# A22's negated copy for the first sum of a pair: made by GpSimd instead of ScalarE

## The chip, the core and the metric

The kernel runs on one core of a Trainium2 chip. The core has a matrix engine (TensorE, PE in the profile), a vector engine (VectorE, DVE), an engine for activations and copies (ScalarE, ACT), a general one (GpSimd, POOL) and a queue that only starts transfers (SyncE, SP). Each works through its own queue of instructions and waits on semaphores for the others. PEld in the profile is the loading of weights into TensorE. Transfers between the main memory and the on-chip memory are issued by SP, ACT or POOL and run beside the engines.

The metric is the device time of one execution in microseconds (us), lower being better.

## What is computed

Two layers of a small transformer work on 256 tokens of an image ("lat") and 256 tokens of context ("cx"), 1024 features each, in float32. The first layer mixes tokens by a short convolution, the second by attention. Before and after the mixer stands a feed-forward network, so there are four; in the second layer the context ends at the attention, and the last network works on the image tokens alone.

```python
def _modulate(t, g, shift, scale):
    return _rms(t, g) * (1 + scale) + shift

def _swiglu(h, w13, w2):
    gte, up = jnp.split(h @ w13, 2, axis=-1)
    return (jax.nn.silu(gte) * up) @ w2
...
    mod = (jax.nn.silu(c) @ mod_w[i] + mod_b[i]).reshape(bsz, 3, 3, 1, D_MODEL)
...
    lat = lat + 0.5 * mod[:, 0, 2] * _swiglu(_modulate(lat, norm_g[i, 0], ...), ffn_w13[i, 0], ffn_w2[i, 0])
```

The change lies in the product `h @ w13` of the first three networks: 1024 features by 2 x 2816 hidden columns.

## The kernel before

**Precision.** A float32 product is made of three TensorE products. Each operand is split into a rounded part "hi" and the rest "lo" (`split`, L107): ACT copies the source with rounding (L108), DVE subtracts that copy from the source (L109). `mm3` (L133) issues hi x hi (L137), hi x lo (L138) and lo x hi (L139) into one accumulator. So each weight tile costs one ACT and one DVE pass before TensorE can use it.

**A network.** `ffn` (L766) works on the 22 blocks of 128 hidden columns in three thirds of 8, 7 and 7. For each block the gate and the up product are made, then silu(gate) * up, and at the end of a third `project` (L575) multiplies the blocks by `w2` and adds the result to the tokens (`finish`, L559). Work of a slower kind runs between: the modulation vectors are made on DVE (L179) in units that the loops hand out (`tick`).

**A pair.** In the first three networks most blocks are made by the class `Pair` with seven products of half-size blocks in place of eight, in the manner of Strassen and Winograd. The weights of a block are cut into A11 and A12 (first half of the features; up and gate columns) and A21 and A22 (second half), the tokens into B blocks and their sums T1 to T4. Two tiles of 128x1024 hold a pair's weights: `r2` gets A22 and A12 by one transfer (through `load_raw`, L104), and the right half of `r1` gets A11 by another (L693). The left half of `r1` is made in two steps: a copy of A22 times -1 (L695), then a transfer that POOL issues, which adds A21 from memory to what lies there (L696). So it holds A21 - A22. `sums(0)` subtracts it from A11 on DVE (L715) and splits both halves into S1 and S2 (`keep`, L703). `sums(1)` makes split copies of A22 itself (`split_far`, L111: two passes on ACT, L113 and L114, and a second adding transfer by POOL, L115), subtracts S2's raw form from both halves of `r2` on DVE (L723), and splits the result into S3 and S4.

The products follow in this order: `head` (A11 and A12; ACT then copies the first product to `sg`, L740), `five` (S1 by T1; ACT copies it to `gm`, L746), `six` (S2 by T2, which adds to the accumulator that L740 copied; S4, which adds to the one that L746 copied), and for the pair before `seven` (S3; DVE L757) and `four` (A22; DVE L763 and the split of the result). There are 56 pairs, and so 56 negations.

**Buffers and order.** Raw weight tiles have 8 buffers ("wr"), split tiles 4 each ("wh" and "wl"), A22's split copies 2 each ("w4h" and "w4l"). A weight buffer is free again when its last reader is done. The order on each engine is written out by hand only for the first stage and for the attention heads (`manual_schedule`); elsewhere a planner of the tile layer places the instructions of several pairs between each other by costs of its own. Loads, negations and adding transfers of later pairs therefore stand in the queues among the products and copies of earlier ones.

**Other users of POOL.** POOL issues the two adding transfers of each pair. In the attention stage, which has no pairs, it also multiplies 128x512 tiles by a scalar (L1300).

Of the kernel before, what the change touches and what calls it, by code (L numbers as in the profile page):

```python
# [12 lines left out]
AF = mybir.ActivationFunctionType  # L13
ALU = mybir.AluOpType
# [6 lines left out]
T2 = 2 * S  # L21
# [26 lines left out]
def hybrid_kernel(ctx: ExitStack, tc: tile.TileContext, a: dict, out: bass.AP):  # L48
    nc = tc.nc
# [12 lines left out]
    def nm(s):  # L62
        uid[0] += 1
        return f"{s}{uid[0]}"
# [15 lines left out]
    for q in range(4):  # L80
# [10 lines left out]
        out=const.tile([P, 1], F32, name="silu", tag="silu"), in_=eps_t, func=AF.Silu  # L91
# [10 lines left out]
    def load_raw(src, n=1024):  # L102
        raw = wp.tile([P, 1024], F32, name=nm("wr"), tag="wr", bufs=8)
        nc.sync.dma_start(raw[:, :n], src)  # L104
        return raw

    def split(hi, lo, src):  # L107
        nc.scalar.activation(out=hi, in_=src, func=AF.Copy)  # L108
        return nc.vector.tensor_tensor(out=lo, in0=src, in1=hi.bitcast(F32), op=ALU.subtract)  # L109
# [7 lines left out]
    def half():  # L117

        return tuple(
            wp.tile([P, 1024], F32R, name=nm(t), tag=t, bufs=4) for t in ("wh", "wl")  # L120
        )
# [198 lines left out]
    class Plain:  # L320


        def __init__(self):
            self.t = [(hot("hh"), hot("hl")) for _ in range(KT // 2)]
# [357 lines left out]
    class Pair:  # L682
# [6 lines left out]
        def __init__(self, src, h):  # L689
            self.h, self.w, self.src = h, {}, src  # L690
            r2 = load_raw(src[:, 1024:2048])
            r1 = wp.tile([P, 1024], F32, name=nm("wr"), tag="wr", bufs=8)
            nc.sync.dma_start(r1[:, T2:], src[:, T2:1024])  # L693

            nc.scalar.activation(out=r1[:, :T2], in_=r2[:, :T2], func=AF.Copy, scale=-1.0)  # L695
            nc.gpsimd.dma_start(out=r1[:, :T2], in_=src[:, :T2], accum_op=ALU.add)  # L696
            self.raw = [r1, r2]
            ts = half()
            for i, key in enumerate(("A11", "A12")):
                self.w[key] = [t[:, i * T2 : i * T2 + T2] for t in ts]  # L700
                split(*self.w[key], self.raw[i][:, T2:])
# [185 lines left out]
    for k in range(KT):  # L887
# [5 lines left out]
        out=sb1, in0=modb[:, 0, KT : 2 * KT], scalar1=1.0, scalar2=None, op0=ALU.add  # L893
# [175 lines left out]
    for m in range(KT):  # L1069
# [4 lines left out]
        for c0, c1 in ((0, S), (S, T2)) if m == 0 else ((0, T2),):  # L1074
# [18 lines left out]
            out=d2[:, :, 1:], in0=u2[:, :, : S - 1], scalar=convk[:, 0, m : m + 1],  # L1093
# [3 lines left out]
            out=d2[:, :, : S - 1], in0=u2[:, :, 1:], scalar=convk[:, 2, m : m + 1],  # L1097
# [152 lines left out]
    for kv in range(KVH):  # L1250
# [8 lines left out]
        out=scq, in0=rq[:, :16], scalar1=float(P) ** -0.5, scalar2=None, op0=ALU.mult  # L1259
# [202 lines left out]
```

## Time and profile before

| | before |
|---|---|
| time, median of 3 runs | 1584.83 us (1580.87 to 1585.39) |
| time of the profiled execution | 1582.14 us |
| its span | 1580.4 us |
| TensorE busy | 1558.5 us, 99% |
| VectorE busy | 1279.5 us, 81% |
| ScalarE busy | 801.8 us, 51% |
| GpSimd busy | 123.1 us, 8% |
| memory traffic | 263.52 MB, mean 167 GB/s |
| mean granted TensorE clock | 0.996 |

How to read the lines quoted below. In the order of time, a line gives its start in us from the start of the span, its length in us, engine, source line, operation, output and inputs, shape and count; brackets at the end tell how long the engine stood idle before it and whose work ended that. In the groups, a line gives line, engine, operation, names, shapes and count, then busy us and mean ns of one, then the idle time before these instructions and what ended it. In the list of waits, the numbers are total us, how often, and the longest. In the view by stretches, a line gives the stretch, its length, the busy us (with the count of instructions) of PE, PEld, DVE, ACT and POOL, the granted TensorE clock, the share of DMA and GB/s. "fp32r" is the rounded form of float32 that the splits produce. Matmuls overlap, so a busy share of PE near 100% says that it hardly waits, not that it runs at its peak.

### The profile page before, as it was taken

How to read it: one execution, taken by the hardware profiler on the slowest of the kernel's cores; microseconds unless marked ns; L12 is line 12 of the kernel's file. 1: busy time of each engine (PE TensorE's matmuls, PEld its weight loads, DVE VectorE, ACT ScalarE, POOL GpSimd, SP SyncE). 2: the span in 40 equal slices, each digit the busy share in tenths (PEclk: the TensorE clock that was granted, in tenths of full speed). 3: DMA queues.
4: the chain of work that ended last, by engine and by line, in shares of the span. 5: the costliest groups of instructions: out<-in, count | busy, mean ns of one | idle time of the engine just before them, and what ended most of it. 6: DMA issues, size and time to landing. Idle time of an engine off the chain costs nothing. (4 is left out here: it accounts for less than half of the span.)

```text
span 1580.4 us, 26335 instructions
## 1 busy us (share of the span) xinstructions
PE 1558.5 (99%) x10282; PEld 1426.4 (90%) x10282; DVE 1279.5 (81%) x2023; ACT 801.8 (51%) x1345; POOL 123.1 (8%) x132
## 2 busy tenths in 40 slices
PE   9999999999999999999999999999999999999999
PEld 7888998999888899989999899989889889898888
DVE  5978789789998678977987988977968887887676
ACT  5643553554332366446446476446445355674553
POOL 0001101100000000011010001011010002300000
PEclk9999999999999999999999999999999999999999
DMA  9667457555565434674665724665865753256562
GB/s 370 211 178 190 117 155 198 130 170 174 182 203 175 134 81 120 190 176 102 201 166 126 215 67 125 202 163 129 243 158 154 244 162 124 91 183 220 166 202 74
DMA packets 88253, 263.52 MB, mean 167 GB/s; under 512 B 10817, under 2 KB 12609, under 8 KB 88129
## 3 DMA queue, kind: packets, MB, share of 16 engines
q1 hardware_dynamic: 69408, 230.72, 45.6%
q0 software_dynamic: 16128, 29.37, 11.3%
q10 hardware_dynamic: 2592, 1.76, 0.4%
q8 instruction: 80, 1.31, 0.3%
q14 instruction: 45, 0.36, 0.1%
HBM read 259.45 MB, written 1.05 MB: 165 GB/s over the span
## 5 line engine op out<-in xcount | busy, mean ns | idle before, releaser
L109 DVE TENSOR_TENSOR wl<-wr,wh 128x1024 fp32r<-128x1024 f32 (+2 forms) x446 | 455.5, 1045 | 144.7 <-ACT wh L108 123.4
L108 ACT ACTIVATE wh<-wr 128x1024 fp32r<-128x1024 f32 (+2 forms) x446 | 394.1, 912 | 245.5 <-PE py L138 79.3
L179 DVE CUSTOM_DVE_ANT_0 junk<-wr,scbc,modb 128x1024 bf16<-128x1024 f32 x222 | 284.5, 1281 | 31.8 <-DMA wr<-in_modT 29.0
L137 PE MATMUL py<-gh,wh 128*128 128x512 f32 (+1 forms) x570 | 214.3, 376 | 0.0
L138 PE MATMUL py<-gl,wh 128*128 128x512 f32 (+1 forms) x570 | 214.0, 375 | 0.0
L139 PE MATMUL py<-gh,wl 128*128 128x512 f32 (+1 forms) x570 | 213.7, 375 | 0.0
L137 PE MATMUL p<-th,wh 128*128 128x256 f32 x448 | 127.3, 284 | 4.6 <-ACT sg L740 4.6
L139 PE MATMUL p<-th,wl 128*128 128x256 f32 x448 | 127.1, 284 | 0.0
L138 PE MATMUL p<-tl,wh 128*128 128x256 f32 x448 | 127.0, 283 | 0.0
L139 PEld LDWEIGHTS py<-gh,wl 128*128 128x128 f32 x570 | 107.9, 189 | 19.2
L137 PEld LDWEIGHTS py<-gh,wh 128*128 128x128 f32 x570 | 108.0, 190 | 18.2
L138 PEld LDWEIGHTS py<-gl,wh 128*128 128x128 f32 x570 | 108.0, 190 | 18.0
L559 DVE SCALAR_TENSOR_TENSOR x<-py,mod,x 128x256 f32<-128x256 f32 x213 | 94.2, 479 | 34.5 <-PE py L139 23.3
L696 POOL DMA_DIRECT2D wr<-in_w x56 | 48.8, 872 | 829.9 <-ACT wr L695 672.5
L695 ACT ACTIVATE wr<-wr 128x512 f32<-128x512 f32 x56 | 35.2, 629 | 117.5 <-DMA wr<-in_w 80.9
L137 PE MATMUL q<-bh,wh 128*128 128x256 f32 x320 | 91.1, 285 | 2.0 <-ACT gm L746 1.6
L139 PE MATMUL q<-bh,wl 128*128 128x256 f32 x320 | 91.0, 284 | 0.6 <-DVE wl L109 0.6
L137 PEld LDWEIGHTS p<-th,wh 128*128 128x128 f32 x448 | 86.1, 192 | 5.4 <-ACT sg L740 5.0
L138 PE MATMUL q<-bl,wh 128*128 128x256 f32 x320 | 90.7, 283 | 0.0
L138 PEld LDWEIGHTS p<-tl,wh 128*128 128x128 f32 x448 | 86.1, 192 | 0.4
L139 PEld LDWEIGHTS p<-th,wl 128*128 128x128 f32 x448 | 86.1, 192 | 0.0
L108 ACT ACTIVATE gh<-gm 128x512 fp32r<-128x512 f32 x66 | 41.3, 625 | 71.6 <-DVE gm L763 68.0
(304 smaller groups left out, 4065.8 us busy)
## 6 DMA issues: line engine op xcount, KB each, us to landing
wr<-in_modT SPq DMA_DIRECT2D x126, 512.0 KB, 4.8
wr<-in_w SPq DMA_DIRECT2D x120, 512.0 KB, 4.6
wr<-in_w2b SPq DMA_DIRECT2D x64, 448.0 KB, 4.1
wr<-in_w2a SPq DMA_DIRECT2D x32, 512.0 KB, 5.0
wr<-in_w SPq DMA_DIRECT2D x56, 256.0 KB, 4.0
wr<-in_w POOLq DMA_DIRECT2D x56, 256.0 KB, 4.9
w4l<-in_w POOLq DMA_DIRECT2D x56, 256.0 KB, 5.9
pm<-in_mod SPq DMA_DIRECT2D x16, 512.0 KB, 10.2
```

What stands on the lines that cost most here:

```text
L108: nc.scalar.activation(out=hi, in_=src, func=AF.Copy)
L109: return nc.vector.tensor_tensor(out=lo, in0=src, in1=hi.bitcast(F32), op=ALU.subtract)
L137: nc.tensor.matmul(ps, wh, mh, start=first, stop=False, **kw)
L138: nc.tensor.matmul(ps, wh, ml, start=False, stop=False, **kw)
L139: nc.tensor.matmul(ps, wl, mh, start=False, stop=last, **kw)
L179: nc.vector.tensor_tensor_reduce(out=junk, in0=raw[j], in1=scbc[:, v, :], scale=0.5 if ch in (2, 8) else 1.0, scalar=modb[:, l, col : col ...
L559: nc.vector.scalar_tensor_tensor(out=x[:, m, s * S : s * S + S], in0=ps[:, o : o + S], scalar=g[:, m, s : s + 1], in1=x[:, m, s * S : s * ...
L695: nc.scalar.activation(out=r1[:, :T2], in_=r2[:, :T2], func=AF.Copy, scale=-1.0)
L696: nc.gpsimd.dma_start(out=r1[:, :T2], in_=src[:, :T2], accum_op=ALU.add)
```

## The change

GpSimd makes the negated copy. The operation (times -1), the operands, the shape and the transfer that adds to it are the same; no wait or buffer is written differently. After it, the negation stands on L695 to L697, and every line behind it is two further down (the adding transfer is L698, L715 becomes L717, and so on).

```diff
             r1 = wp.tile([P, 1024], F32, name=nm("wr"), tag="wr", bufs=8)
             nc.sync.dma_start(r1[:, T2:], src[:, T2:1024])
 
-            nc.scalar.activation(out=r1[:, :T2], in_=r2[:, :T2], func=AF.Copy, scale=-1.0)
+            nc.gpsimd.tensor_scalar(
+                out=r1[:, :T2], in0=r2[:, :T2], scalar1=-1.0, scalar2=None, op0=ALU.mult
+            )
             nc.gpsimd.dma_start(out=r1[:, :T2], in_=src[:, :T2], accum_op=ALU.add)
             self.raw = [r1, r2]
```

## The prediction

> **What bounds the kernel now.** I read the page's engine shares first, then the chain of waits of PE, then the groups of the changed line, then the order of time on ACT, PE and DVE where PE waits.
>
> ```profile
> span 1580.4 us, 26335 instructions
> ...
> PE 1558.5 (99%) x10282; PEld 1426.4 (90%) x10282; DVE 1279.5 (81%) x2023; ACT 801.8 (51%) x1345; POOL 123.1 (8%) x132
> ...
> L695 ACT ACTIVATE wr<-wr 128x512 f32<-128x512 f32 x56 | 35.2, 629 | 117.5 <-DMA wr<-in_w 80.9
> ```
>
> TensorE bounds nearly every stage: it is idle for 1580.4 - 1558.5 = 21.9 us, so no relief of another engine can bring much more. ACT is half idle, and the removed work, 35.2 us, is worth nothing by itself. But the last row says more: ACT stood idle for 117.5 us right ahead of the 56 negations, 80.9 us of them until the weights landed. An engine runs its queue in order, so whatever stands behind a waiting negation waits with it. Who suffers is told by PE's waits:
>
> ```profile
> PE p L137 <- ACT sg L740: 4.6, 2, 2.9
> PE q L137 <- ACT gm L746: 4.0, 4, 1.8
> ```
>
> PE waits twice for the copy of the first product (L740), 2.9 and 1.7 us, and four times for the copy of S1*T1 (L746), 4.0 us in all: 1.8 once, the other three 2.2, or 0.73 each. All stand where a third of a feed-forward network starts its pairs. First place, ACT's order of time, in two stretches:
>
> ```profile
> 269.32 0.63 ACT L695 ACTIVATE wr<-wr 128x512 f32<-128x512 f32 x1 [7.79 <-DMA wr<-in_w]
> 269.86 1.04 ACT L108 ACTIVATE wh<-wr 128x1024 fp32r<-128x1024 f32 x1
> ```
> ```profile
> 277.55 0.63 ACT L695 ACTIVATE wr<-wr 128x512 f32<-128x512 f32 x1 [3.10 <-DMA wr<-in_w]
> 278.09 1.13 ACT L108 ACTIVATE wh<-wr 128x512 fp32r<-128x512 f32 x2
> 280.73 0.63 ACT L695 ACTIVATE wr<-wr 128x512 f32<-128x512 f32 x1 [1.51 <-DVE wl L109]
> 281.27 0.35 ACT L740 COPY sg<-p 128x256 f32<-128x256 f32 x1
> 282.04 1.07 ACT L108 ACTIVATE wh<-wr 128x1024 fp32r<-128x1024 f32 x1 [0.42 <-ACT sg L740]
> 283.01 0.34 ACT L746 COPY gm<-q 128x256 f32<-128x256 f32 x1
> ```
> ```profile
> 278.50 0.28 PE L139 MATMUL q<-th,wl 128*128 128x256 f32 x1
> 281.68 0.39 PE L137 MATMUL p<-th,wh 128*128 128x256 f32 x1 [2.89 <-ACT sg L740]
> ```
>
> The copy at 281.27 stands directly behind two negations of later pairs, each of which waited for its own load; PE needed it at 278.6. After that stall PE also runs slower:
>
> ```profile
> 283.00:287.00 4.00, 4.00 (x22) 3.77 (x21) 3.00 (x3) 1.67 (x4) 0.00 (x0) 0.57 0.78 164
> ```
> ```profile
> 1168.00:1172.00 4.00, 4.00 (x34) 4.00 (x35) 2.68 (x3) 1.13 (x2) 0.00 (x0) 1.00 0.41 134
> ```
>
> These are two stretches of 4 us in the view by stretches, with matmuls in brackets and the granted clock third from the end: at a clock of 0.57 PE issued 22 matmuls of the form of which it issues 34 at 1.00. The 12 missing ones are 12 x 4.00/34 = 1.4 us.
>
> **The change, part by part.**
>
> *Order.* In the built program PE's and SP's orders are unchanged. ACT loses the 56 negations; in a few places the two A22 copies (L113, L114) move by a neighbour. DVE swaps neighbours in three places; I take that at nothing. POOL gains 56 negations, each right ahead of the DMA that adds to its result, and one setup instruction long before the first. The order of POOL's DMAs stays.
>
> *The negation on POOL.* Its nearest row is the attention stage's multiplication of the same shape, with POOL and DVE side by side there:
>
> ```profile
> L1300 POOL TENSOR_SCALAR pn<-e,r x16: 1553/1565/1867, 1331.9 to 1361.9; 128x512 f32<-128x512 f32 x16
> ```
> ```profile
> 1347.48 3.11 POOL L1300 TENSOR_SCALAR pn<-e,r 128x512 f32<-128x512 f32 x2 [0.95 <-PE pt L1313]
> ```
> ```profile
> 1347.89 0.81 DVE L109 TENSOR_TENSOR wl<-wr,wh 128x512 fp32r<-128x512 f32 x1
> ```
> ```profile
> L109 DVE TENSOR_TENSOR wl<-wr,wh 128x512 fp32r<-128x512 f32 x132 | 85.9, 690 | 26.7 <-ACT wh L108 26.5
> ```
> ```profile
> L715 DVE TENSOR_TENSOR wr<-wr 128x512 f32<-128x512 f32 x56 | 38.4, 685 | 1.0 <-DMA wr<-in_w 1.0
> ```
>
> 56 x 1.565 = 87.6 us on an engine that is busy 123.1 of 1580.4. Where ACT started the negation the moment the load landed, the adding DMA now goes out 1.565 - 0.629 = 0.94 us later; where ACT was late, earlier. Its reader is L715, and the last row says that L715 waited for a DMA 1.0 us in all 56 times: the DMA is covered elsewhere, and 0.94 us late costs nothing. For that one wait (the first pair) I bound it by -1.0 and +0.94 and take 0, since POOL needn't wait for ACT's queue there. If the cover were gone everywhere, it would be 56 x 0.94 = 53 us. Behind a waiting negation on POOL stand the adding DMA, which waited for the same load before, and A22's DMA of an earlier pair (L115), already queued behind that one. SP's loads don't pass POOL.
>
> *What DVE loses beside POOL.* The split at 1347.89 ran inside a POOL operation and took 0.81 us; the mean of its form is 0.690. So 0.12 us is lost per such operation, and a negation of 1.565 us can meet two. That is 56 x 0.12 = 6.7 to 56 x 0.24 = 13.4 us of DVE, which is idle for 300.9 us. PE sees it only where DVE is late already: three places, two negations each, 6 x 0.24 = +1.5 us. Bounds: 0, and the lock below.
>
> *What ACT gains, first place.* Without negations the copy L740 runs behind the halves at 278.09 and before PE asks. Late next is the copy L746: it stands behind L108 at 282.04, which reads DVE's L715:
>
> ```profile
> 270.94 1.23 DVE L109 TENSOR_TENSOR wl<-wr,wh 128x1024 fp32r<-128x1024 f32 x1 [2.04 <-ACT wh L108]
> ...
> 280.89 0.69 DVE L715 TENSOR_TENSOR wr<-wr 128x512 f32<-128x512 f32 x1
> ```
>
> If DVE stayed put, PE would stop again 1.44 us (12 matmuls at 0.12) after 278.62, at 280.06, until 283.4, and nothing would be won: that is the lower end, 0. But DVE itself waited 2.04 us for the split at 269.86, behind a negation that sat 7.79 us. Without it L715 moves from 280.89 to 278.85, L108 to 280.0, the copy to 281.0, and PE restarts at 281.4 instead of 283.4: -2.0 us. A wait of 1.3 us in place of 2.9 should leave the clock alone (the second place waits 1.7 us and the stretch from 1168 has 1.00), so -1.4 us more. Together -3.4; the upper end is 2.9 + 0.3 + 1.4 = -4.6.
>
> The Trainium skill (TensorE: Matmul & The Clock Gate, "What's actually happening") says that the clock is halved after an idle window of about 3.4 us which runs freely, so that the same gap may or may not cost it. The trace agrees: 0.57 over 4 us is 3.4 us at half clock. With the window falling otherwise, the sum would lack its 1.4 us.
>
> *Second place.*
>
> ```profile
> 1159.46 0.63 ACT L695 ACTIVATE wr<-wr 128x512 f32<-128x512 f32 x1 [6.41 <-DMA wr<-in_w]
> 1160.00 1.04 ACT L108 ACTIVATE wh<-wr 128x1024 fp32r<-128x1024 f32 x1
> 1163.38 0.63 ACT L695 ACTIVATE wr<-wr 128x512 f32<-128x512 f32 x1 [2.34 <-DVE x L559]
> 1163.92 1.13 ACT L108 ACTIVATE wh<-wr 128x512 fp32r<-128x512 f32 x2
> 1164.95 0.35 ACT L740 COPY sg<-p 128x256 f32<-128x256 f32 x1
> 1166.54 1.06 ACT L108 ACTIVATE wh<-wr 128x1024 fp32r<-128x1024 f32 x1 [1.24 <-issue]
> 1167.51 0.35 ACT L746 COPY gm<-q 128x256 f32<-128x256 f32 x1
> ```
> ```profile
> 1161.07 1.23 DVE L109 TENSOR_TENSOR wl<-wr,wh 128x1024 fp32r<-128x1024 f32 x1 [1.73 <-ACT wh L108]
> 1162.21 0.87 DVE L559 SCALAR_TENSOR_TENSOR x<-py,mod,x 128x256 f32<-128x256 f32 x2
> 1164.56 1.29 DVE L109 TENSOR_TENSOR wl<-wr,wh 128x512 fp32r<-128x512 f32 x2 [1.47 <-ACT wh L108]
> 1165.77 0.69 DVE L715 TENSOR_TENSOR wr<-wr 128x512 f32<-128x512 f32 x1
> ```
>
> The same picture: DVE waits 1.73 + 1.47 = 3.2 us for splits behind negations. With these gone the first copy no longer waits (-1.7), and L715 is 3.2 us earlier, more than the second copy was late (-0.7). Together -2.4; lower end 0, where the halves' buffers hold ACT instead.
>
> *Third place.*
>
> ```profile
> 702.85 1.29 DVE L109 TENSOR_TENSOR wl<-wr,wh 128x512 fp32r<-128x512 f32 x2 [2.13 <-ACT wh L108]
> ```
>
> One of the three waits of 0.73 us for L746 follows it, and 2.13 us of DVE's lateness are ACT's: -0.7, or 0.
>
> *Sum.* -3.4 - 2.4 - 0.7 + 1.5 = -5.0 us. The profiled execution took 1582.14 us (its span is 1580.4), so 1577.1, rounded to 1577. Its own time is 2.7 us under the median of 1584.83, inside the runs' spread of 1580.87 to 1585.39.
>
> **The rivals.**
>
> *The copies are held by something else.* The halves need buffers that PE's last projection frees, and DVE needn't move when ACT does. Then the new waits replace the old ones, DVE's loss is +1.5 at most, and the time is 1581 to 1584. For it: half of each gain hangs on DVE moving. Against it: DVE's waits name ACT in all three places.
>
> *Slower: POOL shuts DVE out.* Should a negation hold off every DVE operation with two inputs in SBUF for its whole length, DVE loses up to 87.6 us. On the average it has room. At the start of a third it hasn't: two negations fall within 4 us there (277.55, 280.73), 3.1 us of DVE, of which a microsecond may be spare. Nine thirds x 2.1 = +19, less nothing gained: about 1601. It decides from (3.4 + 2.4 + 0.7)/9/2 = 0.36 us lost per negation, against 0.12 to 0.24 by the row. Against it: the split at 1347.89 started and ended inside a POOL operation.
>
> The Trainium skill (SBUF — State Buffer, "Who interferes with whom") states just this rule, an exclusive lock for the whole instruction between DVE with two SBUF inputs and a GpSimd read. The trace disagrees in these rows: 0.81 us, not a block.
>
> *The adding DMA becomes late.* It needs the cover of L715 to be under 0.94 us; the 1.0 us in 56 speaks against it. A part of the second rival's chance is for it.
>
> **How the numbers follow.** Forecast 0.57, with a range of its own of 1572 to 1580; copies held otherwise 0.25; slower 0.18. Low end: upper ends of all gains, 4.6 + 2.4 + 0.7, and no loss on DVE give 1574.4; 1571 allows for one of the other short waits of PE. High end 1588 takes in all of the second case and the slight forms of the third, and leaves out the rest. A measurement of this kernel tells about 0.3%, 4.8 us, from no change. Faster by more 0.57, within 0.25, slower 0.18.
>
> **What would show it.** In the profile after: PE's two waits for the copy of p gone or under a microsecond, and no stretch at half clock near 283 us; ACT idle no longer until loads land at negations, with DVE's waits at 271, 703 and 1161 gone; POOL's 56 negations near 1.57 us; splits beside them near 0.81 against 0.69; L715 with no more DMA waits than one. The prediction is wrong if negations on POOL take 2.5 us or more, if DVE's busy time grows by over 20 us, or if PE's waits move to DVE's wl or L757 at the starts of the thirds.

## Result, and the profile after

| | before | after |
|---|---|---|
| median (9 runs each, same chip) | 1582.14 us (1579.19 to 1585.39) | 1572.92 us (1566.72 to 1575.37) |
| ratio after to before | | 0.9933, 95% interval 0.9916 to 0.9950 |
| profiled execution, its span | 1582.14 us, 1580.4 us | 1566.88 us, 1565.1 us |
| granted clock of that execution | 0.996 | 1.000 |

The kernel became faster by 0.7%, 9.2 us between the medians, where 5.0 us were forecast. The profiled execution after is one of the fastest of its nine, so its span flatters the change; how much is worked out below. Two more measurements of the changed kernel, at other times, gave ratios of 0.9938 and 0.9948.

The page of the changed kernel, its first part and the group of the changed line (L695 is the negation, now on POOL):

```profile
span 1565.1 us, 26349 instructions
...
PE 1550.9 (99%) x10282; PEld 1420.6 (91%) x10282; DVE 1284.6 (82%) x2023; ACT 778.7 (50%) x1289; POOL 223.5 (14%) x188
...
L695 POOL TENSOR_SCALAR wr<-wr 128x512 f32<-128x512 f32 x56 | 99.3, 1774 | 718.7 <-DMA wr<-in_w 256.0
```

ACT's busy time fell by 23.1 us, POOL's grew by 100.4 us and DVE's by 5.1 us. (ACT's fell by less than the 35.2 us of the negations, because the records of successive operations overlap: before, the negation at 269.32 ends at 269.95 and the next operation starts at 269.86.) The wait for the loads is now POOL's, 256.0 us, and the first sum on DVE, which reads what stands behind it, waited only 0.3 us in all. PE's waits, the first two rows of the list:

```profile
PE q L137 <- ACT gm L748: 2.7, 3, 2.1
PE ss L274 <- DVE acc L265: 1.5, 1, 1.5
```

The waits for the first product's copy (4.6 us before) are gone, and of the 4.0 us for the second product's copy 2.7 are left, 2.1 of them at the first pairs of the kernel, where before too it waited 1.8. The first place, in the order of time on ACT and PE (compare the rows from 277.55 to 283.01 before):

```profile
275.31 1.06 ACT L108 ACTIVATE wh<-wr 128x1024 fp32r<-128x1024 f32 x1 [2.92 <-DVE wr L717]
276.27 0.35 ACT L748 COPY gm<-q 128x256 f32<-128x256 f32 x1
```
```profile
276.68 0.39 PE L137 MATMUL q<-hh,wh 128*128 128x256 f32 x1 [0.38 <-ACT gm L748]
```

Nothing stands ahead of the copy but the halves, and PE waits 0.38 us for it. At the second place (1159 to 1168 before), the copies leave when PE's product is done:

```profile
1159.97 1.15 ACT L108 ACTIVATE wh<-wr 128x512 fp32r<-128x512 f32 x2 [0.43 <-PE q L138]
1161.53 0.37 ACT L748 COPY gm<-q 128x256 f32<-128x256 f32 x1 [0.41 <-PE q L139]
```

The granted clock, by stretches of 20 us, without the last one, which the end of the kernel cuts off. In the profiled execution before these four of the stretches were under 0.99; after, none was. The second fence is the stretch from 283 to 287 us after, the third the two stretches under 0.99 in a repeat of the changed kernel:

```profile
0.00:20.00 20.00, 18.63 (x136) 16.43 (x137) 8.11 (x29) 10.71 (x20) 0.19 (x4) 0.91 0.92 332
100.00:120.00 20.00, 18.19 (x132) 17.69 (x131) 18.07 (x26) 9.05 (x14) 0.00 (x0) 0.91 0.48 154
280.00:300.00 20.00, 18.32 (x139) 18.10 (x140) 12.68 (x17) 11.21 (x21) 2.61 (x3) 0.91 0.45 96
1260.00:1280.00 20.00, 17.70 (x123) 16.78 (x122) 14.69 (x33) 9.14 (x16) 0.00 (x0) 0.91 0.49 163
```
```profile
283.00:287.00 4.00, 4.00 (x36) 4.00 (x35) 2.81 (x4) 1.54 (x3) 2.37 (x2) 1.00 0.07 14
```
```profile
100.00:120.00 20.00, 18.01 (x127) 17.35 (x126) 18.07 (x26) 9.37 (x14) 0.00 (x0) 0.91 0.54 162
1260.00:1280.00 20.00, 18.99 (x139) 18.31 (x140) 16.44 (x37) 11.58 (x23) 0.00 (x0) 0.91 0.43 129
```

The stretch from 283 to 287, quoted in the prediction at 0.57, lost 4.00 x 0.43 = 1.7 us to half clock, which is the 0.09 x 20 = 1.8 us of a stretch of 20 us. So each such drop costs some 1.7 us. Four of them before, none in this execution after, two in the repeat (span 1570.0 us): without the drops the spans are 1580.4 - 6.9 = 1573.5, 1565.1 and 1570.0 - 3.4 = 1566.6 us. The change itself is worth 7 to 8 us of waits, and 1.7 us for the drop at 283, which followed PE's longest wait there. The other three drops cannot be put down to the change: two of them are there again in the repeat of the changed kernel.

### The profile page after: what moved, and what is told of

Read it like the earlier page. It is cut to its first block, busy times and chain, and to the rows that moved or that the text cites. A ratio compares the mean times of both kernels' runs of the same rounds, so it can differ in the third digit from the quotient of the medians.

```text
span 1565.1 us, 26349 instructions
## 1 busy us (share of the span) xinstructions
PE 1550.9 (99%) x10282; PEld 1420.6 (91%) x10282; DVE 1284.6 (82%) x2023; ACT 778.7 (50%) x1289; POOL 223.5 (14%) x188
## 4 chain that ended last, share of the span: by engine, by line
PE 86%; DVE 8%; issue 2%; ACT 2%; DMA 2%; POOL 0%; POOLq 0%; DVEq 0%; ACTq 0%; SPq 0%
PE py L137 7%; PE py L138 7%; PE py L139 7%; PE p L137 6%; PE p L139 6%; PE p L138 6%; PE q L137 5%; PE q L139 5%; PE q L138 5%; PE py L145 2%; PE pg L145 2%; PE pu L145 2%; DVE junk L179 2%; DVE wl L109 2%; DMA wr<-in_modT 1%
## 5 line engine op out<-in xcount | busy, mean ns | idle before, releaser
L695 POOL TENSOR_SCALAR wr<-wr 128x512 f32<-128x512 f32 x56 | 99.3, 1774 | 718.7 <-DMA wr<-in_w 256.0
L559 DVE SCALAR_TENSOR_TENSOR x<-py,mod,x 128x256 f32<-128x256 f32 x213 | 94.0, 476 | 41.3 <-PE py L139 29.9
L115 POOL DMA_DIRECT2D w4l<-in_w x56 | 53.1, 948 | 271.8 <-ACT w4l L114 197.6
## 6 DMA issues: line engine op xcount, KB each, us to landing
wr<-in_w SPq DMA_DIRECT2D x56, 256.0 KB, 4.1
wr<-in_w POOLq DMA_DIRECT2D x56, 256.0 KB, 5.0
w4l<-in_w POOLq DMA_DIRECT2D x56, 256.0 KB, 6.0
```

The lines of the kernel that those rows point to most:

```text
L115: nc.gpsimd.dma_start(out=lo, in_=src, accum_op=ALU.add)
L559: nc.vector.scalar_tensor_tensor(out=x[:, m, s * S : s * S + S], in0=ps[:, o : o + S], scalar=g[:, m, s : s + 1], in1=x[:, m, s * S : s * ...
L695: nc.gpsimd.tensor_scalar(out=r1[:, :T2], in0=r2[:, :T2], scalar1=-1.0, scalar2=None, op0=ALU.mult)
```

## Experiments

Ratios are to the kernel before on the same chip, with 95% intervals. The rows make three groups of four, each run together on one chip with the kernel before: it took 1582.72 us beside the first group, 1581.08 us beside the second and 1583.3 us beside the third.

| run | median, us | ratio | without half clock, us |
|---|---|---|---|
| the change, repeated | 1570.72 | 0.9938 (0.9918 to 0.9958) | 1567.1 |
| a sliver of the negation on ACT | 1581.18 | 0.9997 (0.9978 to 1.0016) | 1572.0 |
| the change, another ACT copy doubled | 1578.52 | 0.9980 (0.9965 to 0.9994) | 1573.1 |
| the change, negation made twice | 1575.63 | 0.9956 (0.9941 to 0.9971) | 1568.9 |
| negation on ACT, behind the pair two before | 1570.33 | 0.9926 (0.9900 to 0.9952) | 1565.0 |
| negation on DVE | 1593.71 | 1.0074 (1.0047 to 1.0102) | 1578.5 |
| both negations of a pair on POOL | 1579.86 | 0.9990 (0.9972 to 1.0008) | 1573.9 |
| only the second negation on POOL | 1594.78 | 1.0080 (1.0052 to 1.0109) | 1580.8 |
| the change, repeated | 1573.48 | 0.9948 (0.9930 to 0.9966) | 1566.2 |
| on ACT, behind the pair two before | 1570.26 | 0.9926 (0.9908 to 0.9945) | 1565.5 |
| on ACT, behind the pair three before | 1575.91 | 0.9949 (0.9929 to 0.9968) | 1569.5 |
| on ACT, behind the pair just before | 1723.82 | 1.0887 (1.0866 to 1.0908) | 1669.6 |

The last column leaves the half clock out: it is the median, over the executions, of the span times its mean granted clock (which is given to 0.001, or 1.6 us). The kernel before has 1574.1, 1574.4 and 1574.5 us there in the three groups, and the nine executions of the changed kernel above have 1566.9. So some 7 to 8 us of the gain are waits, in every measurement; the rest of each difference is how often the clock dropped.

By the traces, PE's operations stand in the order of before in all of these runs but two: the doubled copy (15 places differ) and the place behind the pair just before (39 places). There the planner also moved over a hundred operations on ACT and as many on DVE, so these two runs test more than their edits say.

**Is it the wait or the work?** The changed kernel was first measured again.

> The changed kernel once more, as the base on this chip. Both theories: ratio to before 0.992 to 0.995. On the clock: an execution whose mean granted clock is 1.000 should stand near 1567 us, those at 0.996 to 0.998 near 1573, since a drop lasts 3.4 us at half clock and so costs 1.7 us, and 0.004 of 1571 us is 6.3 us.

Measured 1570.72 us, ratio 0.9938. What was expected of the clock is not borne out one by one: the execution with a mean of 1.000 took 1569.2 us, and the three at 0.997 took 1570.3 to 1573.7. Then ACT was given back 8 of the 512 columns, at its old place in the queue; POOL negates the other 504.

```diff
+            nc.scalar.activation(out=r1[:, :8], in_=r2[:, :8], func=AF.Copy, scale=-1.0)
             nc.gpsimd.tensor_scalar(
-                out=r1[:, :T2], in0=r2[:, :T2], scalar1=-1.0, scalar2=None, op0=ALU.mult
+                out=r1[:, 8:T2], in0=r2[:, 8:T2], scalar1=-1.0, scalar2=None, op0=ALU.mult
             )
```

> ScalarE negates 8 of the 512 columns, at the places where it negated all of them before; GpSimd negates the other 504. So ScalarE's queue waits for the same loads as before the change, but its work there is a third or less. Theory 'the wait': what the change won was the queue behind a waiting negation, so the gain goes: ratio to before 0.998 to 1.002 (1579 to 1585 us), and PE waits again for the copy of the first product (L743), about 4 us in all. Rival 'the work': what was won is ScalarE's 35 us of busy time; with 0.2 us per sliver two thirds of it stay won, ratio 0.993 to 0.996.

Measured 1581.18 us: the whole gain is gone. Without the half clock 1572.0 us is left, so 4.9 of 7.0 us are lost to waits and the rest to more drops (mean granted clock 0.9951, against 0.9982 in the repeat). The sliver waits for loads for 88.9 us in 32 times, as the negation did for 80.9 in 28, while the first sum waits for its transfer for 0.7 us, once. ACT's order of time and the list of PE's waits (L743 and L749 are the two copies here):

```profile
277.55 0.21 ACT L695 ACTIVATE wr<-wr 128x8 f32<-128x8 f32 x1 [3.48 <-DMA wr<-in_w]
277.66 1.14 ACT L108 ACTIVATE wh<-wr 128x512 fp32r<-128x512 f32 x2
280.58 0.21 ACT L695 ACTIVATE wr<-wr 128x8 f32<-128x8 f32 x1 [1.77 <-DVE wl L109]
280.70 0.35 ACT L743 COPY sg<-p 128x256 f32<-128x256 f32 x1
```
```profile
PE q L137 <- ACT gm L749: 3.7, 2, 2.8
PE ss L274 <- DVE acc L265: 3.1, 2, 1.9
PE p L137 <- ACT sg L743: 2.8, 2, 2.4
```

An operation of 0.21 us that waits for a load holds the copy behind it as the whole negation of 0.63 us did. The wait in the queue is enough, without most of the 35.2 us of work. This agrees with the first part of the prediction.

**Is ACT's work free there?** In the changed kernel the copy L113 was made twice.

```diff
         nc.scalar.activation(out=hi, in_=raw, func=AF.Copy)
+        nc.scalar.activation(out=hi, in_=raw, func=AF.Copy)
```

> The changed kernel, but ScalarE makes A22's rounded copy twice in a row (56 more operations of 0.63 us, 35 us of work, behind a wait that is there anyway). ScalarE is then as busy as before the change, without the negation's own wait. Theory 'the wait': the gain stays, ratio 0.992 to 0.996. Rival 'the work': the gain goes, ratio 0.998 to 1.002.

Measured 1578.52 us, ratio 0.9980: above the theory's range, which missed, and at the lower end of the rival's. PE waits elsewhere than before:

```profile
PE q L140 <- DVE wl L109: 4.3, 8, 1.4
PE q L138 <- ACT gm L749: 2.5, 3, 1.8
```

Eight waits for splits on DVE are new (the changed kernel and its repeats have one of them at most), and DVE waited 27.0 us for A22's second copy, for which it did not wait in the changed kernel. But the planner answered this edit with another order on PE, ACT and DVE, so how much of the loss is the doubled work is open. "Worth nothing by itself" is shown for the negation's own place and not for any work on ACT.

**Is DVE's loss beside POOL felt?** The changed kernel made its negation twice on POOL.

```diff
             nc.gpsimd.tensor_scalar(
                 out=r1[:, :T2], in0=r2[:, :T2], scalar1=-1.0, scalar2=None, op0=ALU.mult
             )
+            nc.gpsimd.tensor_scalar(
+                out=r1[:, :T2], in0=r2[:, :T2], scalar1=-1.0, scalar2=None, op0=ALU.mult
+            )
```

> The changed kernel with the negation made twice in a row by GpSimd. It doubles what GpSimd takes from VectorE through a shared way to memory: VectorE's busy time grew by 5 us with 56 negations (1279.5 to 1284.6) and should reach about 1290. Theory 'the loss is covered': PE sees under 1 us of it, ratio 0.992 to 0.996. Rival 'VectorE's loss reaches PE at the starts of the thirds': another 1.5 us or more, ratio 0.995 or above. The adding transfer goes out 1.5 us later, which its cover of 3 us and more should take everywhere but in the first pair.

Measured 1575.63 us, 4.9 us over the repeat of the change. DVE's busy time grew by 12 us, to 1297.1, and PE's waits for the second copy came back at the starts of thirds:

```profile
PE q L137 <- ACT gm L751: 7.3, 5, 3.1
```

The largest, 3.1 us, is at the first pairs of the kernel, where the changed kernel waits 2.1. The order on PE, ACT and DVE is that of the changed kernel, and the first sum waited for the adding transfer only once, 1.6 us; what is left to explain the waits is DVE's loss. So that loss is not wholly covered: of the 12 us added, 4.9 us reached PE by the medians, and 1.8 us without the half clock. (51 of the 54 pairs of runs have the doubled negation slower; the intervals of the two ratios overlap.)

**Is it the engine or the place in the queue?** The negation stays on ACT, but is issued behind the second copy (`gm`) of the pair two before. POOL then has no computing to do in these stages, and ACT keeps all of its work. The list of copies runs on over the ends of thirds and networks, so only the first two pairs of the whole kernel stay where the planner puts them, not the first two of each third, as the expectation has it.

```diff
+    copies = []
...
-            nc.scalar.activation(out=r1[:, :T2], in_=r2[:, :T2], func=AF.Copy, scale=-1.0)
+            with tc.issue_after(copies[-2]) if len(copies) >= 2 else nullcontext():
+                nc.scalar.activation(out=r1[:, :T2], in_=r2[:, :T2], func=AF.Copy, scale=-1.0)
...
-            nc.scalar.copy(self.gm[:, S:], self.q1)
+            copies.append(nc.scalar.copy(self.gm[:, S:], self.q1).ins)
```

> The kernel before, the negation still on ScalarE and as long (56 x 0.63 us), but each queued behind the second copy (L749) of the pair two before it. So it no longer stands ahead of copies that TensorE needs soon; only the first two pairs of a third stay where the planner puts them. Theory 'the wait ahead of the copies': the gain is had without GpSimd, ratio to before 0.990 to 0.995, and no loss on VectorE beside it (its busy time near 1279). Rival 'it must leave ScalarE': ratio 0.998 to 1.002. A second rival: the adding transfer now goes out so late that VectorE waits for it (L717 by more than 5 us in all), ratio above 1.000.

Measured 1570.33 us, ratio 0.9926: all of the gain, with ACT at 807.9 us busy. From what the negation waited for (us, times), and PE's first wait:

```profile
  DMA wr<-in_w: 13.3, 7
```
```profile
PE q L137 <- ACT gm L749: 2.7, 1, 2.7
```

Its waits for loads fell from 80.9 us in 28 times to 13.3 in 7. DVE's order is that of before, and on ACT little more than the negations moved. GpSimd isn't what helps; the place is.

**The other engine.** The negation on DVE (`nc.vector` in place of `nc.gpsimd` in the changed kernel):

> The negation on VectorE instead, the order of TensorE, ScalarE and SP otherwise as in the changed kernel. Theory 'the wait': VectorE's queue now waits for the loads, ahead of splits that TensorE needs, and it is the busier engine (81% against 51%), so ratio 1.000 to 1.010, with TensorE waiting for VectorE's splits. Rival 'any engine but ScalarE will do': 0.992 to 0.997.

Measured 1593.71 us, as the theory forecast, but not by the wait that it named. From PE's waits and DVE's:

```profile
PE q L137 <- ACT gm L748: 19.0, 5, 6.7
```
```profile
DVE wr L717 <- DMA wr<-in_w: 18.7, 4, 6.3
DVE wr L695 <- DMA wr<-in_w: 15.0, 16, 2.2
```

PE waits for the second copy and hardly for splits (1.0 us, once), and the four longest of its waits (6.7, 4.3, 3.3 and 4.5 us) each follow, by 14 to 19 us, a wait of the first sum for the adding transfer (6.3, 4.3, 4.9 and 3.2 us). POOL can issue that transfer only when DVE has made the negation, so at the starts of thirds it goes out too late. The waits for loads ahead of the negations are shorter, 15.0 us in 16 times. Without the half clock the run is 4.1 us over the kernel before; the rest of the 12.6 us is drops (mean granted clock 0.9917 against 0.9967). So not any other engine will do.

**The other negation.** A22's second split copy (L114), which ACT makes from L113 without a load, was moved to POOL, with the change and without it.

```diff
-        nc.scalar.activation(out=lo, in_=hi.bitcast(F32), func=AF.Copy, scale=-1.0)
+        nc.gpsimd.tensor_scalar(
+            out=lo, in0=hi.bitcast(F32), scalar1=-1.0, scalar2=None, op0=ALU.mult
+        )
```

> The changed kernel with the second negation too (A22's rounded copy times -1, L114, 56 x 0.63 us) on GpSimd. The run with that place's work doubled lost about 7 us against the changed kernel, by waits of TensorE for splits at the ends of the thirds; taking 0.63 us of a pair away at the same place should win some of it: theory 'that place is tight', -2 to -5 us against the changed kernel, ratio 0.989 to 0.993. Against it stands another 12 us of VectorE's time, as in the run with two negations on GpSimd, which cost 5 us there: rival 'the loss on VectorE outweighs', ratio 0.994 to 0.998.

> Only the second negation (L114) on GpSimd; the first stays on ScalarE as before. ScalarE loses the same 35 us of work as by the change, but its waits for loads at L695 stay. Theory 'the wait': most of the gain is not had, ratio 0.997 to 1.002. Rival 'the work': as by the change, 0.992 to 0.995.

Measured 1579.86 us with both on POOL and 1594.78 with the second alone, which is slower than any of the expectations. Both missed. In the second, PE's waits for ACT remain, since the negation still clogs ACT, and waits for DVE come on top:

```profile
PE p L139 <- ACT sg L742: 5.3, 3, 3.8
PE q L139 <- ACT gm L748: 5.0, 7, 2.2
...
PE q L141 <- DVE wl L109: 2.0, 1, 2.0
```

The negation on ACT still waits for loads there, 89.8 us in 34 times. DVE was busy for 1303.6 and 1293.3 us, against 1284.6 and 1279.5 without the move: as in the run that negates twice, POOL takes time from DVE, and here no waiting operation leaves ACT's queue in return. That this is the whole cause is not shown; the move also changed ACT's order in some 20 other places. Of the 13.7 us that it costs without the change, 6.4 are waits and the rest half clock (mean granted clock 0.9925 against 0.9967).

**How late may the negation be?** Last, the place on ACT was varied, beside the changed kernel.

> The changed kernel once more, on the chip of the three runs beside it. Both theories: 1570 to 1573 us, ratio 0.993 to 0.994.

> The negation on ScalarE, behind the second copy of the pair two before. Theory (the place in the queue alone gives the gain, and GpSimd costs VectorE something): 1569 to 1571 us, 1 to 2 us under the changed kernel, since VectorE loses nothing and TensorE's waits are as few. Rival (the two ways are the same, and the 0.4 us by which they differed before was chance): the two intervals cover each other and the medians lie within 1 us.

> The same, behind the second copy of the pair three before, so earlier in ScalarE's queue. If the negations then wait for their loads again at the starts of thirds, the waits of TensorE for the first and second copy come back and the time is 1575 to 1581 us; if the loads land before that place, it is as the run behind the pair two before, 1569 to 1572 us.

> The same, behind the second copy of the pair just before, so later. The negation waits for no load then, but the adding transfer goes out a pair later. Theory (the transfer is still covered): 1569 to 1572 us. Rival (its cover of about 6 us is used up): VectorE's first sum waits for the transfer in most pairs, some 56 times by up to 3 us, and the time is above 1590 us.

The repeat took 1573.48 us (ratio 0.9948), half a microsecond above what was expected; the place three before took 1575.91 us, as expected if the negations wait for their loads again, and the place just before 1723.82 us, the rival's case.

| negation on ACT, behind the second copy of | negation waits for loads, us (times) | first sum on DVE waits for the adding transfer, us (times) | median, us |
|---|---|---|---|
| nothing (before) | 80.9 (28) | 1.0 (1) | 1583.3 |
| the pair three before | 38.0 (13) | 1.2 (1) | 1575.91 |
| the pair two before | 13.6 (7) | 1.9 (2) | 1570.26 |
| the pair just before | 1.0 (2) | 176.7 (48) | 1723.82 |

The time follows the first column down, until the second one opens. The group of the first sum in the last of these runs, and PE's waits:

```profile
L718 DVE TENSOR_TENSOR wr<-wr 128x512 f32<-128x512 f32 x56 | 38.7, 691 | 176.7 <-DMA wr<-in_w 176.7
```
```profile
PE q L137 <- ACT wh L108: 55.9, 36, 3.7
PE q L139 <- DVE wl L109: 41.4, 39, 1.9
```

Those two waits make 97.3 us, and the granted clock of 0.969 over the span of 1723.3 us, against 0.997 in the run two pairs before, some 49 more: together 146 us of the 154 by which the span is longer than that run's 1568.8. By the landings in the traces, the adding transfer was there 22.5 us (median) ahead of the first sum before, 14.8 behind the pair three before and 4.9 behind the pair two before; one pair more uses this cover up. The planner's other order in this run may have its part in the 154 us; it was not tested apart. This is the rival "the adding DMA becomes late": the prediction priced it at 53 us for transfers that are 0.94 us late, and here DVE waited 3.7 us for each of 48.

The version behind the pair two before was faster than the changed kernel by 3.2 us of the medians on this chip (1570.26 against 1573.48; of the 36 pairs of runs 28 are in its favour). The expected 1 to 2 us lie nearer to that than the rival's 1 us, but the intervals, 0.9908 to 0.9945 and 0.9930 to 0.9966, overlap: that it beats the changed kernel is likely and not settled, and without the half clock they are 0.7 us apart. It beats the kernel before in both measurements.

## Why the prediction was right, and where its sizes were off

The cause was right: a negation that waits for its load at the head of ACT's queue holds the copies that PE needs. The sliver shows that the wait does it, and the later place in ACT's queue that the negation need not leave ACT. The size was off: 1572.92 us lies 0.9 us above the low end of the forecast's own range of 1572 to 1580, and the 5.0 us forecast are little more than half of the 9.2 measured.

*First place, forecast -3.4 us.* The prediction said that the second copy would be late next, with a wait of 1.3 us at an undisturbed clock. In the second repeat of the changed kernel just that stands:

```profile
280.13 0.38 PE L137 MATMUL q<-hh,wh 128*128 128x256 f32 x1 [1.29 <-ACT gm L748]
```

In the profiled execution it was 0.38 us. So 2.89 us of waiting became 0.38 to 1.29, and with the drop of 1.7 us gone (forecast 1.4) the place gave -3.3 to -4.2 us. DVE moved with ACT, as the forecast's -2.0 needed: its first sum started 2.27 us behind the point where PE asks for the first copy before, 0.24 us ahead of it in the profiled execution after and 0.67 us behind it in the repeat, so it came 2.5 and 1.6 us nearer.

*Second place, forecast -2.4; third, -0.7.* Neither has a wait left. What PE loses at a wait, from start to start of its matmuls, was 1.83 + 1.02 = 2.85 us and 0.93 us: a little more than the idle times that the forecast added up (1.7 + 0.7, and 0.73).

*Waits that the sum left out.* Two short ones went as well in the profiled execution, and are the larger part of what the forecast gains lacked. In PE's order of time before:

```profile
230.25 0.38 PE L137 MATMUL q<-hh,wh 128*128 128x256 f32 x1 [0.59 <-ACT gm L746]
```
```profile
1228.00 0.39 PE L139 MATMUL q<-bh,wl 128*128 128x256 f32 x1 [0.55 <-DVE wl L109]
```

From start to start they cost 0.75 and 0.71 us. The first is the third of the 0.73 us waits that the prediction named and gave no term; the second names DVE, and the prediction looked only at waits that named ACT, though DVE's splits wait for ACT's. The first is gone in both repeats too. The second is back in one of them, with 0.8 us, so it is not surely the change's.

*DVE's loss, forecast +1.5.* DVE's busy time grew by 5.1 us, less than the 6.7 to 13.4 us forecast, and the sum of the gains above, (3.3 to 4.2) + 2.85 + 0.93 + 1.46 = 8.5 to 9.4 us, less some 0.7 us by which PE waits longer at the first pairs and newly at 806 us, is near the measured 9.2. A cost of 1.5 us would still fit: the runs with the negation late on ACT, where DVE loses nothing, are 0.4 us (across two groups) and 3.2 us (within one) faster than repeats of the change, or 2.1 and 0.7 us without the half clock. The step that failed here is the reading of one split of 0.81 us as "not a block". That split began 0.41 us into POOL's operation, so its 0.12 us are only the end of the time for which POOL holds DVE. The rows of the kernel after (from the view of one line) show how much one operation lost at most:

```profile
L717 DVE TENSOR_TENSOR wr<-wr x56: 677/683/1101, 82.8 to 1203.5; 128x512 f32<-128x512 f32 x56
L695 POOL TENSOR_SCALAR wr<-wr x56: 1479/1614/2530, 74.0 to 1173.7; 128x512 f32<-128x512 f32 x56
```

The lowest, median and longest first sum on DVE: at worst 0.42 us over the median, not 0.12. The negation has 1.77 us in the mean, not 1.57, and 2.53 at worst, past the 2.5 us that the forecast named as a sign against it: for single ones, and not for their mean.

*The rivals.* The copies were not held by something else. POOL does shut DVE out, though not for a whole negation: DVE's operations beside the 56 negations, and the attention stage's 16 multiplications, took 7.3 us more than the medians of their forms, 0.13 us for each at most, under the 0.36 us from which that rival decided. Twice the negations brought part of the added loss to PE, 1.8 to 4.9 us of 12, so this rival stood nearer than the prediction thought. The adding DMA stayed covered (the first sum waited 0.3 us, once); with the negation one pair too late on ACT it was not, in 48 of 56 pairs.

*The half clock.* The prediction took it from one stretch that a wait of 1.7 us leaves the clock alone. That the drop at 283 went is in its favour, but other waits of that size show that it was partly luck: the execution before waited 1.81 us at the first pairs and then had a granted clock of 0.72 from 104 to 110 us, and the one after waited 2.06 us there and had 1.00. The execution before had four drops, and only the one at 283 entered the sum. Executions of one kernel differ by such drops, at about 13, 104 and 1260 to 1277 us: the fastest of the changed kernel, 1566.7 us, and the slowest, 1575.4, are 8.7 us apart, and their granted clocks of 1.000 and 0.996 make 6.3 of these.

## What to carry to other kernels

An instruction that waits for a load on an in-order queue costs what stands behind it, and not its own length: look for it at the short copies that the bounding engine asks for, and price it by their lateness. Such work can be moved to an idle engine, but issuing it later on the same engine did as well here, without the other engine's side effects. Of the three places tried, the best was the latest one from which its own reader is still covered; one step later that reader waited 176.7 us. Another engine is no help if the work stands late in its queue, as on DVE here. When short waits of the bounding engine go back to the same engine through a second one, count those too.

## What the runs showed of the hardware that was not expected

GpSimd's negation and a VectorE operation that reads two tiles which TensorE did not write shut each other out, but not for equal times. In the changed kernel, in the order of time on POOL and DVE:

```profile
148.49 2.44 POOL L695 TENSOR_SCALAR wr<-wr 128x512 f32<-128x512 f32 x1 [1.79 <-DMA wr<-in_w]
...
282.84 1.65 POOL L695 TENSOR_SCALAR wr<-wr 128x512 f32<-128x512 f32 x1 [5.06 <-DMA wr<-in_w]
```
```profile
148.35 1.22 DVE L725 TENSOR_TENSOR wr<-wr,wr 128x1024 f32<-128x1024 f32 x1
...
281.84 1.29 DVE L109 TENSOR_TENSOR wl<-wr,wh 128x512 fp32r<-128x512 f32 x2 [2.12 <-ACT wh L108]
283.05 1.10 DVE L717 TENSOR_TENSOR wr<-wr 128x512 f32<-128x512 f32 x1
```

The negation at 148.49 began 0.14 us into a DVE operation of 1.22 us and took 2.44 us: 1.08 us until DVE was done, and 1.36, near its shortest time of 1.48. The one at 282.84 met the end of a split (0.29 us), took 1.65 us, again 1.36 more, and the next operation on DVE took 1.10 us in place of 0.68: it was held for 0.42 us of the negation, and ran through the rest of it. So GpSimd waits for the whole of such a DVE operation in progress, and DVE waits for GpSimd for some 0.4 us: 0.43 us is the most in this execution, 0.48 in the second repeat. A DVE operation with an input that TensorE wrote does not hold GpSimd: the negation at 1129.49 met one (L559) with 0.45 us to go and took 1.49 us. The Trainium skill (SBUF — State Buffer, "Who interferes with whom") has the one that comes first hold the shared port for its whole instruction; the trace agrees where DVE is first, and disagrees where GpSimd is: 0.42 us of 1.65.

The drops to half clock cost 1.7 us each and are most of the spread between runs of this kernel, 6.3 of 8.7 us between the fastest and the slowest. The Trainium skill (TensorE: Matmul & The Clock Gate, "What's actually happening") has them come with a window that runs freely; the drops that came and went at the same places, between executions of one kernel, agree with it.
